# A decoder mixer step: memory prepared ahead of the x chunks, with constant matmuls on the scaled memory tiles

## The chip, the cores and the metric

One core of one Trainium2 chip runs the whole program. The metric is device time in microseconds (us) of one execution; a profiled execution gives the trace that the rows below come from.

## The reference

One layer of a hybrid mixer over 2048 prompt tokens and 8 x 4 sample tokens of width 1024:

```python
xn = rmsnorm(x, g_pre)
proj = xn @ w_in
a_c, b_c, g_c, x_r, g_r, q, g_q = split(proj)
mn = rmsnorm(mem, g_mem)                      # 256 memory tokens
mem_k, mem_v = mn @ w_mem_k, mn @ w_mem_v     # (256, 512) each
u = a_c * sigmoid(b_c)                        # conv group: depthwise conv of 31 taps, layernorm, silu
c = silu(layernorm(conv31(u))) * silu(g_c)
h = linear_recurrence(gates(conv4(x_r)))      # RG-LRU group
rr = h * silu(g_r)
o = softmax(q @ mem_k.T / sqrt(128)) @ mem_v * silu(g_q)
y = x + rmsnorm(concat(c, rr, o) @ w_out, g_post)
```

Keys and values of the memory are outputs too. Every product is made of three matmuls on split operands (high x high, high x low, low x high), in `mm3`.

## The kernel before

Phase 1 computes all projections in two parts of 1024 tokens; part 0 also carries the 32 sample tokens. A part is cut into chunks of 352, 352 and 320 tokens (the last has 352 columns with the samples). Phase 2 multiplies by `w_out`.

For part 0 the x rows come in as tiles of up to 128 rows (`chunk_rows`, three tiles a chunk, from the pool behind `big`). `norm_rows` takes the mean square of a tile on ScalarE (`row_rs`, L212), the power on GpSimd (L214) and scales the tile on VectorE (L220). `transposed` turns each 128-column block on TensorE (L227) into a PSUM bank of `ps_q`, which has four; ScalarE writes the high part (L229), VectorE the low part (L230), and the bank is free again. A projection (`proj`) loads one weight tile of 512 KB (`load_w`), splits it on ScalarE (L108) and VectorE (L109), and runs 24 matmuls for each chunk (L103 to L105). The raw weight tile `wr` has two buffers (`WR = 2`), and so have `wh` and `wl`: a third weight can be loaded when the first has been split.

The memory path is `mem_prep` (two tiles of 128 rows, the same norm, 16 transposes), `mem_k(h)` for four heads (a weight tile each, 24 matmuls of 256 columns) and `mem_v` (four weight tiles, 12 matmuls of 512 columns each, into two banks of `ps_q` that are held to the end).

Work is written in the order of the token string `ORDER`: G is a conv pair's projections and the convolution on VectorE, N, M and V are memory, X and S the recurrence, C, O, q, o gates and attention, L small constants, R row statistics. The Tile scheduler then places the instructions of all engines, by priority and by its own clock; each engine runs its list in that order. The x chunks of part 0 are prepared in a loop ahead of the string, and `G0` (weights 6 and 0, `FIRST` and `M_A`) follows. `WARM` gives 18 matmuls on a constant tile at the very start.

Of the kernel before, what the change touches and what calls it, by code (L numbers as in the profile page):

```python
# [16 lines left out]
P = 128  # L17
# [27 lines left out]
GRP = 2  # L45
NPB = 6
ORDER = (
    "G0 N M1 M0 M2 L X0 G1 G2:3 V G2 S0:2 S0:1 M3 S0:1 S0 C0 O0 C1 q0 G3 o0 R X1:7 X1 S1:1 G4 S1:1 S1:1 C2 C4 S1 O1 q1 o1 G5 q3 C3 q2 o2 o3 C5",
    "G0:1 G0 s0 s1 p v0 X0 v1 G1 S0:1 G2:1 S0:1 G2 S0:1 S0 C0 O0 q0 o0 G3 G4:3 X1 S1:1 G4 S1:1 S1 C1 O1 q1 G5 o1 q3 q2 o3 o2 C5 C4 C2 C3",
)  # L50
PART = 1024
SB8 = PART // P
WARM = 18
XRW = LH + PART + NB * (LH + NS)
M_A, M_B, M_GC, M_XR, M_GR, M_Q, M_GQ = 0, 6, 12, 18, 24, 30, 34
FIRST = M_B
# [11 lines left out]
def hybrid_mixer_kernel(ctx, tc, x, xT, mem, consts, lnc, ccT, lcT, ckT, cv, w_in,  # L68
# [3 lines left out]
    act, dve, pe, pool, sp = nc.scalar, nc.vector, nc.tensor, nc.gpsimd, nc.sync  # L72
# [21 lines left out]
    def bank(pl, w=512):  # L94
        t = pl.tile([P, 512], F32, tag="b", name="bk")
        return t[:, :w]

    warm = bank(ps_q, P)
    for _ in range(WARM):
        pe.matmul(warm, ones, ones, start=True, stop=True)  # L100

    def mm3(ps, lh, ll, rh, rl, first, last):
        pe.matmul(ps, lh, rh, start=first, stop=False)  # L103
        pe.matmul(ps, lh, rl, start=False, stop=False)  # L104
        pe.matmul(ps, ll, rh, start=False, stop=last)  # L105

    def split(hi, lo, src):
        act.activation(hi, src, AF.Copy)  # L108
        dve.tensor_tensor(lo, src, hi.bitcast(F32), op=ALU.subtract)  # L109
# [6 lines left out]
    def phase1():  # L116
# [17 lines left out]
        def lc(dt=F32):  # L134
            return pl.tile([P, 3, CW], dt, tag="lc", name="lc")
# [4 lines left out]
        def xslot(dt=F32):  # L140
            return pr.tile([P, XRW], dt, tag="xr", name="xr")

        cst = c1.tile([P, CST_W], F32, name="cst")

        def view(name, pat=None, **kw):
            o, w = CST[name]
            v = cst[:, o:o + w]
            return v.rearrange(pat, **kw) if pat else v
# [5 lines left out]
        V = {n: view(n) for n in VEC}  # L154
# [53 lines left out]
        def row_rs(t, n, junk):  # L208

            ms = pt.tile([P, 1], F32, tag="ms", name="ms")  # L210
            rs = pt.tile([P, 1], F32, tag="rs", name="rs")
            act.activation(junk()[:n, :D], t[:n, :D], AF.Square, accum_out=ms[:n, :])  # L212
            dve.tensor_scalar(rs[:n, :], ms[:n, :], 1.0 / D, EPS, op0=ALU.mult, op1=ALU.add)
            pool.tensor_tensor(rs[:n, :], rs[:n, :], mhalf[:n, 0:1], op=ALU.pow)  # L214
            return rs

        def norm_rows(tiles, junk):
            for t, n in tiles:
                rs = row_rs(t, n, junk)
                dve.tensor_scalar(t[:n, :D], t[:n, :D], rs[:n, :], None, op0=ALU.mult)  # L220

        def transposed(tiles, g, hi, lo):
            for k in range(KD):
                ps = bank(ps_q, sum(n for _, n in tiles))
                c0 = 0
                for t, n in tiles:
                    pe.transpose(ps[:, c0:c0 + n], t[:n, k * P:(k + 1) * P], ident[:n, :n])  # L227
                    c0 += n
                act.activation(hi(k), ps, AF.Copy, scale=g[:, k:k + 1])  # L229
                dve.scalar_tensor_tensor(lo(k), ps, g[:, k:k + 1], hi(k).bitcast(F32),  # L230
                                         op0=ALU.mult, op1=ALU.subtract)

        def load_w(src, ahead=None):
            with tc.high_priority(offset=W_HIGH if ahead is None else ahead):
                raw = pw.tile([P, KD, P], F32, tag="wr", name="wr", bufs=WR)
                sp.dma_start(raw, src)
                wh = pw.tile([P, KD, P], F32R, tag="wh", name="wh")
                wl = pw.tile([P, KD, P], F32R, tag="wl", name="wl")
                split(wh, wl, raw)
            return wh, wl  # L240
# [5 lines left out]

        def mem_prep():
            tiles = load_rows([[mem[i * P:(i + 1) * P, :]] for i in range(2)], flat_lc)
            norm_rows(tiles, xslot)
            mn = [lc(F32R).rearrange("p a b -> p (a b)")[:, :4 * NMEM].rearrange("p (a b) -> p a b", a=4)  # L250
                  for _ in range(4)]
            memn["hi"] = lambda k: mn[k // 4][:, k % 4, :]
            memn["lo"] = lambda k: mn[2 + k // 4][:, k % 4, :]
            transposed(tiles, gm, memn["hi"], memn["lo"])

        def mem_k(h):
            hi, lo = memn["hi"], memn["lo"]
            kv = pg.tile([P, 8, P], F32R, tag="g", name="kv")
            wh, wl = load_w(w_mem[h])
            ps = bank(ps_p, NMEM)  # L260
            for k in range(KD):
                mm3(ps, wh[:, k, :], wl[:, k, :], hi(k), lo(k), k == 0, k == KD - 1)
            f = ck()[:, :NMEM]
            act.activation(f, ps, AF.Copy)
            st_.dma_start(nkT[h], f)
            flat = lambda a: kv[:, a:a + 2, :].rearrange("p a b -> p (a b)")
            split(flat(0), flat(2), f)
            pool.dma_start(kvd[h][:, :4, :], kv[:, :4, :])

        def mem_v():  # L270

            hi, lo = memn["hi"], memn["lo"]
            ps = [bank(ps_q) for _ in range(2)]
            for i in range(HEADS):
                wh, wl = (t.rearrange("p a b -> p (a b)") for t in load_w(w_mem[HEADS + i]))
                for c in range(2):
                    cs = slice(c * P, (c + 1) * P)
                    for kk in range(2):
                        k = 2 * i + kk
                        ws = slice(kk * 512, kk * 512 + 512)  # L280
                        mm3(ps[c], hi(k)[:, cs], lo(k)[:, cs], wh[:, ws], wl[:, ws], k == 0, k == KD - 1)
                yield
            for c in range(2):
                f = big()[:, :512]
                act.activation(f, ps[c], AF.Copy)
                st_.dma_start(nv[c], f)
                kv = pg.tile([P, 8, P], F32R, tag="g", name="kv")
                split(kv[:, :4, :], kv[:, 4:, :], f.rearrange("p (h d) -> p h d", h=HEADS))
                for a in range(2):
                    pool.dma_start(kvd[:, :, 4 + 2 * a + c, :].rearrange("h p d -> p h d"), kv[:, 4 * a:4 * a + 4, :])  # L290
# [3 lines left out]
        for part in range(2):  # L294
            chunks = []
            for c0 in range(0, PART, CW):
                n = min(CW, PART - c0)
# [16 lines left out]
        def chunk_rows(part, c):  # L314
            return load_rows([[x[t:t + w, :] for _, w, t in b] for b in row_blocks(part, c)], big)
# [40 lines left out]
        for part in range(2):  # L356
            t0 = part * PART
            has_s = part == 0
            chunks = part_chunks[part]

            xh, xl = [], []
            ready = {}
            rows = {}
            if has_s:
                rows[0] = chunk_rows(0, 0)
                sp.dma_start(cst, consts)
            ready[FIRST] = load_w(w_in[FIRST], 0)
            for c, (c0, n, ns) in enumerate(chunks):
                h = px.tile([P, KD, CW], F32R, tag="xh", name="xh")
                l = px.tile([P, KD, CW], F32R, tag="xl", name="xl")  # L370
                w = n + ns
                hi, lo = (lambda k: h[:, k, :w]), (lambda k: l[:, k, :w])
                if has_s:
                    if c + 1 < len(chunks):
                        rows[c + 1] = chunk_rows(0, c + 1)
                    if c == 0:
                        ready[M_A] = load_w(w_in[M_A], 0)
                    norm_rows(rows[c], xslot)
                    transposed(rows.pop(c), gp, hi, lo)
                else:  # L380
                    split_cols(scaled_cols(part, c), gp, hi, lo)
                xh.append(h)
                xl.append(l)
            def proj(m, evac):
                wh, wl = ready.pop(m) if m in ready else load_w(w_in[m])
                for c, (c0, n, ns) in enumerate(chunks):
                    w = n + ns
                    ps = bank(ps_p, w)
                    for k in range(KD):
                        mm3(ps, wh[:, k, :], wl[:, k, :], xh[c][:, k, :w], xl[c][:, k, :w],  # L390
                            k == 0, k == KD - 1)
                    evac(c, ps)
                    yield
# [402 lines left out]
            for tok in ORDER[part].split():  # L796
                name, _, cnt = tok.partition(":")
# [252 lines left out]
```

## Time and profile before

| what | us |
|---|---|
| median of 3 runs | 1433.07 (1430.61 to 1433.35) |
| the profiled execution, its own time | 1434.65 |
| its span, first to last instruction | 1432.8 |
| TensorE (PE) busy | 1409.8 |
| VectorE (DVE) busy | 1097.3 |
| ScalarE (ACT) busy | 675.3 |
| GpSimd (POOL) busy | 158.4 |

A matmul's end is modelled and overlaps the next one, so TensorE's busy time hides a slow pace. What tells more is the count of matmuls in a stretch beside its length, and the granted clock there. The span lies 1.85 us below the execution's own time, which lies 1.58 us above the median.

### The profile page before, as it was taken

The numbers are of one execution on the slowest core, as the hardware profiler recorded it, in microseconds if no ns is written. First come the engines' busy times: TensorE is split into PE (matmuls) and PEld (weight loads), VectorE is DVE, ScalarE is ACT, GpSimd is POOL, SyncE is SP. The second block draws the span as 40 slices with busy tenths as digits, with TensorE's granted clock in tenths as the row PEclk, the third lists the DMA queues.
The fourth block names the chain that finished last, engine by engine and source line by source line (L and its number), as shares of the span: only waits on it lengthen the run. The fifth ranks groups of instructions, "written<-read, shape, count | busy, mean of one in ns | idle before, by whom it ended". The sixth has DMA issues, their size and how long they took to land. (4 is left out here: it accounts for less than half of the span.)

```text
span 1432.8 us, 20977 instructions
## 1 busy us (share of the span) xinstructions
PE 1409.8 (98%) x8346; PEld 1317.6 (92%) x8346; DVE 1097.3 (77%) x1481; ACT 675.3 (47%) x1314; POOL 158.4 (11%) x233
## 2 busy tenths in 40 slices
PE   8999999999999999999999999999999999999998
PEld 7899999999999999899999999999986788888886
DVE  6796995989978989599989997899864645545442
ACT  6423787336754335237842369434453432423321
POOL 2100222011210101012100121000100000000000
PEclk9999999999999999999999999999999999999999
DMA  7343526132252213631122211421474333324320
GB/s 225 110 46 89 140 90 227 42 93 72 85 188 75 65 60 111 219 123 66 54 104 65 75 54 60 162 74 53 154 238 128 96 121 124 125 85 140 98 86 30
DMA packets 102658, 152.24 MB, mean 106 GB/s; under 512 B 21368, under 2 KB 72176, under 8 KB 102560
## 3 DMA queue, kind: packets, MB, share of 16 engines
q1 hardware_dynamic: 89904, 118.66, 27.3%
q0 software_dynamic: 12656, 32.25, 6.7%
q8 instruction: 65, 1.06, 0.3%
q14 instruction: 33, 0.27, 0.1%
HBM read 114.84 MB, written 36.04 MB: 105 GB/s over the span
## 5 line engine op out<-in xcount | busy, mean ns | idle before, releaser
L103 PE MATMUL bk<-xh,wh 128*128 128x352 f32 (+1 forms) x1824 | 585.4, 322 | 2.1 <-ACT xh L229 1.3
L104 PE MATMUL bk<-xl,wh 128*128 128x352 f32 (+1 forms) x1824 | 585.2, 321 | 0.0
L105 PE MATMUL bk<-xh,wl 128*128 128x352 f32 (+1 forms) x1824 | 583.1, 321 | 0.0
L455 DVE SCALAR_TENSOR_TENSOR big<-ub,cst,big 128x1024 f32<-128x1024 f32 x360 | 457.4, 1284 | 8.5 <-issue 3.8
L104 PEld LDWEIGHTS bk<-xl,wh 128*128 128x128 f32 x1824 | 344.3, 189 | 2.7 <-issue 1.6
L103 PEld LDWEIGHTS bk<-xh,wh 128*128 128x128 f32 x1824 | 342.9, 188 | 4.2 <-ACT xh L229 1.9
L105 PEld LDWEIGHTS bk<-xh,wl 128*128 128x128 f32 x1824 | 343.2, 188 | 1.7 <-issue 1.0
L104 PE MATMUL bk<-wol,mh 128*128 128x512 f32 x512 | 201.1, 393 | 0.4 <-DVE wol L109 0.4
L103 PE MATMUL bk<-woh,mh 128*128 128x512 f32 x512 | 199.8, 392 | 0.0
L105 PE MATMUL bk<-woh,ml 128*128 128x512 f32 x512 | 199.4, 391 | 0.0
L108 ACT ACTIVATE wh<-wr 128x1024 fp32r<-128x1024 f32 x84 | 89.0, 1060 | 129.5 <-PE bk L104 113.7
L109 DVE TENSOR_TENSOR wl<-wr,wh 128x1024 fp32r<-128x1024 f32 x84 | 102.9, 1226 | 27.0 <-ACT wh L108 26.7
L105 PEld LDWEIGHTS bk<-woh,ml 128*128 128x128 f32 x512 | 96.2, 188 | 19.8 <-issue 0.8
L104 PEld LDWEIGHTS bk<-wol,mh 128*128 128x128 f32 x512 | 96.2, 188 | 19.6 <-DVE wol L109 0.8
L103 PEld LDWEIGHTS bk<-woh,mh 128*128 128x128 f32 x512 | 96.2, 188 | 19.4
L881 ACT ACTIVATE cr<-cr,lnv 128x128 f32<-128x128 f32 (+1 forms) x102 | 40.7, 477 | 151.1 <-DVE cr L879 151.1
L569 ACT ACTIVATE lc<-bk,hb 128x352 f32<-128x352 f32 (+3 forms) x144 | 77.3, 545 | 31.4 <-PE bk L105 29.3
L542 DVE SCALAR_TENSOR_TENSOR lc<-xr,cst,lc 128x352 f32<-128x352 f32 (+2 forms) x126 | 61.0, 521 | 7.2 <-ACT lc L538 7.1
L879 DVE TENSOR_TENSOR cr<-cr,bk 128x768 f32<-128x768 f32 (+1 forms) x17 | 15.6, 918 | 57.7 <-PE bk L878 57.7
L921 DVE TENSOR_TENSOR o<-bk,gpb 128x512 f32<-128x512 f32 (+1 forms) x34 | 23.3, 686 | 37.4 <-ACT sqj L920 37.4
L920 ACT ACTIVATE sqj<-bk 128x512 f32<-128x512 f32 (+1 forms) x34 | 20.1, 591 | 51.1 <-PE bk L105 50.8
L490 ACT ACTIVATE xr<-bk 128x352 f32<-128x352 f32 (+1 forms) x36 | 16.1, 450 | 56.4 <-PE bk L105 50.1
(238 smaller groups left out, 1693.6 us busy)
## 6 DMA issues: line engine op xcount, KB each, us to landing
wr<-in_w_in SPq DMA_DIRECT2D x76, 512.0 KB, 3.8
mr<-mixd SPq DMA_DIRECT2D x16, 1024.0 KB, 5.6
raw<-in_w_out SPq DMA_DIRECT2D x16, 512.0 KB, 4.6
xt<-in_x SPq DMA_DIRECT2D x16, 512.0 KB, 5.4
out_y<-xt SPq DMA_DIRECT2D x15, 512.0 KB, 2.7
convd<-big POOLq DMA_DIRECT2D x12, 512.0 KB, 3.7
mixd<-big POOLq DMA_DIRECT2D x12, 512.0 KB, 5.3
cr<-convd SPq DMA_DIRECT2D x16, 384.0 KB, 4.8
```

Source lines behind the costliest of these rows:

```text
L103: pe.matmul(ps, lh, rh, start=first, stop=False)
L104: pe.matmul(ps, lh, rl, start=False, stop=False)
L105: pe.matmul(ps, ll, rh, start=False, stop=last)
L108: act.activation(hi, src, AF.Copy)
L109: dve.tensor_tensor(lo, src, hi.bitcast(F32), op=ALU.subtract)
L455: dve.scalar_tensor_tensor(acc[:, :PART], ub[:, j:j + PART], cw[:, i, j:j + 1], acc[:, :PART], op0=ALU.mult, op1=ALU.add)
L490: act.activation(xb[:, LH + c0:LH + c0 + n], ps[:, :n], AF.Copy)
L542: dve.scalar_tensor_tensor(o, src(j), lw[:, ch, j:j + 1], o, op0=ALU.mult, op1=ALU.add)
L569: act.activation(dst[lo_:hi_, i, :], ps[lo_:hi_, :], AF.Tanh, scale=0.5, bias=hb[lo_:hi_, a, 3 * g + i:3 * g + i + 1])
L881: act.activation(cr[:, i, :], cr[:, i, :], AF.Silu, scale=lng[:, i:i + 1], bias=lnb[:, i:i + 1])
L920: act.activation(sqj[:m, :], ps[n][:m, :], AF.Square, scale=float(D ** -0.5), accum_out=ms[:m, n:n + 1])
L921: dve.tensor_tensor(o[:m, ns], ps[n][:m, :], gpb[:m, ns], op=ALU.mult)
```

## The change

The tokens N, M0 to M3 and V leave `ORDER`. A written order stands in their place ahead of the string in part 0: constants, memory rows, x rows of chunk 0, keys 0 and 1, x rows of chunk 1, chunk 0, keys 2 and 3, x rows of chunk 2, half the values, chunk 1, the rest of the values, the two weights of `G0`, chunk 2. `norm_rows` takes `keep`; for the memory tiles it issues five matmuls of 128 columns on each scaled tile into the bank of the start's constant matmuls, whose result nobody reads.

```diff
-    "G0 N M1 M0 M2 L X0 G1 G2:3 V G2 S0:2 S0:1 M3 S0:1 S0 C0 O0 C1 q0 G3 ...
+    "G0 L X0 G1 G2:3 G2 S0:2 S0:1 S0:1 S0 C0 O0 C1 q0 G3 ...
...
+KEEP = 5
...
-        def norm_rows(tiles, junk):
+        def norm_rows(tiles, junk, keep=0):
             for t, n in tiles:
                 rs = row_rs(t, n, junk)
                 dve.tensor_scalar(t[:n, :D], t[:n, :D], rs[:n, :], None, op0=ALU.mult)
+                for _ in range(keep):
+                    pe.matmul(warm, t[:n, :P], t[:n, :P], start=True, stop=True)
...
         def mem_prep():
             tiles = load_rows([[mem[i * P:(i + 1) * P, :]] for i in range(2)], flat_lc)
-            norm_rows(tiles, xslot)
+            norm_rows(tiles, xslot, KEEP)
...
-            if has_s:
-                rows[0] = chunk_rows(0, 0)
-                sp.dma_start(cst, consts)
-            ready[FIRST] = load_w(w_in[FIRST], 0)
-            for c, (c0, n, ns) in enumerate(chunks):
+
+            def x_chunk(c):
+                c0, n, ns = chunks[c]
...
-                    if c + 1 < len(chunks):
-                        rows[c + 1] = chunk_rows(0, c + 1)
-                    if c == 0:
-                        ready[M_A] = load_w(w_in[M_A], 0)
                     norm_rows(rows[c], xslot)
                     transposed(rows.pop(c), gp, hi, lo)
...
+            if has_s:
+                sp.dma_start(cst, consts)
+                mem_prep()
+                rows[0] = chunk_rows(0, 0)
+                mem_k(0)
+                mem_k(1)
+                rows[1] = chunk_rows(0, 1)
+                x_chunk(0)
+                mem_k(2)
+                mem_k(3)
+                rows[2] = chunk_rows(0, 2)
+                vals = mem_v()
+                next(vals)
+                next(vals)
+                x_chunk(1)
+                for _ in vals:
+                    pass
+                for m in (FIRST, M_A):
+                    ready[m] = load_w(w_in[m])
+                x_chunk(2)
+            else:
+                ready[FIRST] = load_w(w_in[FIRST], 0)
+                for c in range(len(chunks)):
+                    x_chunk(c)
```

The scheduler places everything anew. Three places show what became of the order.

SyncE's list of transfers at the start, before (`big` are x tiles, `lc` the memory tiles, `cst` the constants, `wr` weights; L203 loads rows, L236 weights):

```order
L203 DMA big<-in_x 128x1024 x2
L203 DMA big<-in_x 96x1024
L366 DMA cst<-in_consts 128x304
L236 DMA wr<-in_w_in 128x1024
L203 DMA big<-in_x 128x1024 x2
L203 DMA big<-in_x 96x1024
L236 DMA wr<-in_w_in 128x1024
L409 DMA ub<-in_ccT 128x8x30
L203 DMA lc<-in_mem 128x1024 x2
```

and now:

```order
L383 DMA cst<-in_consts 128x304
L204 DMA lc<-in_mem 128x1024 x2
L204 DMA big<-in_x 128x1024 x2
L204 DMA big<-in_x 96x1024
L239 DMA wr<-in_w_mem 128x1024 x2
L204 DMA big<-in_x 128x1024 x2
L204 DMA big<-in_x 96x1024
L432 DMA ub<-in_ccT 128x8x30 x3
L239 DMA wr<-in_w_mem 128x1024 x5
L204 DMA big<-in_x 128x1024 x2
L204 DMA big<-in_x 64x1024
L204 DMA big<-in_x 32x1024
```

The first projection weight was the fifth transfer; now it follows all eight memory weights and all x rows.

ScalarE's list at the start, before (L212 squares a tile, L108 splits a weight, L229 writes a transposed block):

```order
L212 ACTIVATE xr,ms<-big 128x1024 x2
L212 ACTIVATE xr,ms<-big 96x1024
L165 ACTIVATE spt<-spt 128x6
L108 ACTIVATE wh<-wr 128x1024
L212 ACTIVATE xr,ms<-big 128x1024
L229 ACTIVATE xh<-bk,cst 128x352 x4
```

and now (L213, L109 and L232 are the same three):

```order
L213 ACTIVATE xr,ms<-lc 128x1024 x2
L213 ACTIVATE xr,ms<-big 128x1024 x2
L213 ACTIVATE xr,ms<-big 96x1024
L232 ACTIVATE lc<-bk,cst 128x256 x4
L109 ACTIVATE wh<-wr 128x1024
L232 ACTIVATE lc<-bk,cst 128x256
L109 ACTIVATE wh<-wr 128x1024
```

The squares of the three x tiles of chunk 0 now stand between the memory's squares and the first block that is written from its transposes.

TensorE's list at the start, before (L100 the constant matmuls, L227 transposes, then projections):

```order
L100 MATMUL bk<-ones 128x128 x18
L227 MATMUL bk<-ident,big 128x128 x8
L227 MATMUL bk<-ident,big 128x96 x4
L103 MATMUL bk<-xh,wh 128x352
```

and now (L223 the ten new matmuls, L230 transposes, L104 to L106 the keys):

```order
L101 MATMUL bk<-ones 128x128 x18
L223 MATMUL bk<-lc 128x128 x5
L230 MATMUL bk<-ident,lc 128x128 x3
L223 MATMUL bk<-lc 128x128 x5
L230 MATMUL bk<-ident,lc 128x128 x11
L104 MATMUL bk<-lc,wh 128x256
L105 MATMUL bk<-lc,wh 128x256
L230 MATMUL bk<-ident,lc 128x128 x2
```

The first matmuls that count are now 256 columns wide and belong to the memory's keys.

## Rows read from the trace of the kernel before

**Rows 1.** The page: TensorE's share, and its busy tenths in 40 slices.
```profile
PE 1409.8 (98%) x8346; PEld 1317.6 (92%) x8346; DVE 1097.3 (77%) x1481; ACT 675.3 (47%) x1314; POOL 158.4 (11%) x233
PE   8999999999999999999999999999999999999998
```
**Rows 2.** Stretches of the start: length, then each engine's busy time (instructions); granted clock; DMA.
```profile
0.00:11.00 11.00, 7.06 (x44) 6.40 (x44) 3.42 (x18) 5.89 (x9) 2.68 (x12) 1.00 0.82 284
11.00:18.00 7.00, 6.00 (x23) 5.19 (x24) 6.72 (x25) 6.85 (x14) 1.92 (x3) 0.51 1.07 300
18.00:52.00 34.00, 31.39 (x208) 29.41 (x207) 23.13 (x60) 21.14 (x44) 3.43 (x6) 1.00 0.40 99
52.00:55.40 3.40, 3.40 (x18) 3.40 (x17) 3.40 (x6) 1.31 (x3) 0.57 (x1) 0.50 0.65 199
55.40:61.00 5.60, 4.04 (x32) 3.63 (x31) 4.88 (x6) 2.97 (x6) 0.58 (x1) 1.00 0.00 0
```
**Rows 3.** TensorE's waits, whole kernel: sum, times, longest (us).
```profile
PE bk L227 <- DVE big L220: 3.0, 2, 2.1
PE bk L105 <- DVE xr L663: 2.8, 2, 2.1
PE bk L904 <- DVE mh L109: 2.7, 1, 2.7
```
**Rows 4.** Timeline of the start: start, duration, instruction, idle before it and its end.
```profile
4.03 1.06 ACT L212 ACTIVATE xr<-big 128x1024 f32<-128x1024 f32 x1 [2.01 <-DMA big<-in_x]
...
8.33 1.06 ACT L212 ACTIVATE xr<-big 96x1024 f32<-96x1024 f32 x1 [1.86 <-DMA big<-in_x]
...
11.15 1.06 ACT L212 ACTIVATE xr<-big 128x1024 f32<-128x1024 f32 x1 [0.29 <-DMA big<-in_x]
...
12.79 0.66 PE L103 MATMUL bk<-xh,wh 128*128 128x352 f32 x1 [0.70 <-ACT xh L229]
```
**Rows 5.** Groups by shape from 0 to 61 us: busy, mean ns, idle before.
```profile
L103 PE MATMUL bk<-xh,wh 128*128 128x352 f32 x49 | 15.5, 346 | 2.1 <-ACT xh L229 1.3 <-ACT wh L108 0.7
L227 PE MATMUL bk<-ident,big 128*128 128x128 f32 x48 | 9.9, 295 | 2.7 <-DVE big L220 2.1 <-DVE xl L230 0.5
L212 ACT ACTIVATE xr<-big 128x1024 f32<-128x1024 f32 x6 | 6.4, 1060 | 4.0 <-DMA big<-in_x 3.8
L108 ACT ACTIVATE wh<-wr 128x1024 fp32r<-128x1024 f32 x6 | 6.3, 1054 | 2.8 <-PE bk L104 2.6 <-DMA wr<-in_w_in 0.2
L109 DVE TENSOR_TENSOR wl<-wr,wh 128x1024 fp32r<-128x1024 f32 x5 | 6.1, 1221 | 1.2 <-ACT wh L108 1.1
L100 PE MATMUL bk<-ones 128*128 128x128 f32 x36 | 5.8, 334 | 1.1 <-POOL ones L85 1.1
L103 PE MATMUL bk<-lc,wh 128*128 128x256 f32 x17 | 5.5, 331 | 1.0 <-ACT wh L108 0.8 <-ACT lc L229 0.2
L229 ACT ACTIVATE lc<-bk,cst 128x256 fp32r<-128x256 f32 x8 | 3.5, 489 | 6.0 <-PE bk L227 6.0
```
**Rows 6.** A dense stretch of 160 to 240 us, as in Rows 2.
```profile
160.00:240.00 80.00, 80.00 (x502) 79.85 (x501) 65.55 (x104) 67.43 (x116) 14.74 (x19) 1.00 0.42 131
```
**Rows 7.** Timeline of TensorE, three pairs of starts: transposes, keys, values.
```profile
22.58 0.46 PE L227 MATMUL bk<-ident,big 128*128 128x128 f32 x3
22.82 0.41 PE L104 MATMUL bk<-xl,wh 128*128 128x352 f32 x1
...
57.31 0.28 PE L103 MATMUL bk<-lc,wh 128*128 128x256 f32 x1
...
57.67 0.28 PE L103 MATMUL bk<-lc,wh 128*128 128x256 f32 x1
...
132.26 0.39 PE L103 MATMUL bk<-wh,lc 128*128 128x512 f32 x1
...
132.96 0.40 PE L103 MATMUL bk<-wh,lc 128*128 128x512 f32 x1
```
**Rows 8.** Weight loads of L236 in 0 to 80 us, from issue to landing.
```profile
DMA to landing us min/median/max: 3.7/6.4/11.4
```

More of the change, by code (lines that the diff above doesn't have):

```diff
@@ L47 @@
 ORDER = (
-    "G0 N M1 M0 M2 L X0 G1 G2:3 V G2 S0:2 S0:1 M3 S0:1 S0 C0 O0 C1 q0 G3 o0 R X1:7 X1 S1:1 G4 S1:1 S1:1 C2 C4 S1 O1 q1 o1 G5 q3 C3 q2 o2 o3 C5",
+    "G0 L X0 G1 G2:3 G2 S0:2 S0:1 S0:1 S0 C0 O0 C1 q0 G3 o0 R X1:7 X1 S1:1 G4 S1:1 S1:1 C2 C4 S1 O1 q1 o1 G5 q3 C3 q2 o2 o3 C5",
     "G0:1 G0 s0 s1 p v0 X0 v1 G1 S0:1 G2:1 S0:1 G2 S0:1 S0 C0 O0 q0 o0 G3 G4:3 X1 S1:1 G4 S1:1 S1 C1 O1 q1 G5 o1 q3 q2 o3 o2 C5 C4 C2 C3",
```

## The prediction

> **What bounds the kernel now.** The page comes first: TensorE is busy 98% of the span and 9 tenths or more in 38 of 40 slices [rows 1]. That number flatters it, since a matmul's recorded time overlaps the next one's, so I read the pace instead. In a dense stretch 502 matmuls fill 80 us, 0.159 us each for 352 columns [rows 6]. Three matmuls of the keys take 0.36 us, 0.120 each; three of the values 0.70 us, 0.233 each; a triple of transposes 0.24 us, 0.08 each [rows 7].
>
> Then the stretches of the start. From 0 to 61 us I count the work that is done, at that pace: six projection blocks of `G0` (two weights, three chunks, 24 matmuls: 144; the row counts 49 firsts of three, the last of which starts the next step) give 144 x 0.159 = 22.9; the memory's first keys, 50 matmuls (two heads and two more; 17 firsts in the row), 6.0; 24 triples of x transposes (48 wide ones in the row) 5.8; 16 memory transposes 1.3 [rows 5, 7]. The sum is 36.0 us of work in 60.8, so TensorE is **24.8 us late** when the start is over. Of these, 12.8 pass before the first matmul that counts [rows 4]; the clock is at 0.51 from 11 to 18 us and at 0.50 from 52 to 55.4, its lower level of 1.2 GHz, and there a busy engine gains half a microsecond per microsecond [rows 2]. The second dip and the holes after it fall on the memory step: 4.04 busy of 5.6, with a weight's split and its blocks awaited [rows 2, 5].
>
> Beyond the start little is lost: three waits hold 8.5 us together, one of them of the start [rows 3]. So what the change can move lies in the first 61 us, and at most 24.8 us of it.
>
> **What it removes and adds.** Nothing of the computation goes; 96 key and 48 value matmuls only move. Added are ten constant matmuls. At the start 18 such took 5.8 us, 0.32 each [rows 5], so ten cost 3.2 us if nothing hides them. They stand behind each memory tile's scaling, while ScalarE still squares x tiles, so I take 0; 3.2 is the other end, and a gain through the clock is a rival below.
>
> **The new start, step by step.** SyncE now issues constants, memory, three x tiles, then key weights. The third x tile is the sixth transfer, with as many bytes ahead of it as the sixth had before, which ended ScalarE's wait at 11.15 [rows 4]. ScalarE squares all three x tiles ahead of the first memory block. With the tile before it, the third square ends at some 12.5 (1.06 each and a read of the sum). Four blocks of 0.49 end at 14.5, the first weight's split of 1.05 at 15.5, a block at 16.0, the second split at 17.1 [rows 5]. TensorE's list has two matmuls of the first weight, two transposes, then two of the second: it is dense from 17.1, not from 12.8. By then 16 transposes and two matmuls are done, 1.5 us: 15.6 late.
>
> Between the constant matmuls and 17.1 TensorE has as little to do as it had before its first dip, so I expect 1.2 GHz from about 14 to 21 us, a dip as long as the first [rows 2]. Of that some 4 us are busy: 2 us more. Keys 0 and 1 and five triples end near 25, 17.6 late.
>
> Then each weight needs 1.05 us of ScalarE, 1.22 of VectorE and, through two buffers, at best 3.7 us to land [rows 5, 8]: 6.0 a pair by itself, against 24 x 0.120 = 2.9 or 12 x 0.233 = 2.8 us of TensorE for each weight, 5.7 a pair, and triples between. This pace nearly fits. I add 1.6 us for the waits where ScalarE, full from 8 to 49 us with nine squares, ten splits, 24 x blocks and the evacuations, hands over late. The values end at 46.1: done are 96 x 0.120 = 11.5, 48 x 0.233 = 11.2, memory transposes 1.3 and 12 triples 2.9, together 26.9, so 19.2 late. By then the first projection weight is split (landing 42.5, as the ninth weight, two turns behind the values' third), and `M_A` follows at 50, when 24 matmuls of chunk 0 are behind it. For the remaining blocks of chunks 1 and 2 I add 1.0.
>
> **The sum:** late before 24.8, now 20.2, a gain of 4.6 us. The rest I put at nothing: the string runs the same work, its convolutions only begin some 20 us later, and VectorE had 14.5 us free in 80 in a full stretch [rows 6]. If that cover is gone, a wait such as the one on `xr` at 2.8 us [rows 3] comes back once or twice: 0 to 5.6 us more, or 2.8 less if the new order removes the one there is. Against the profiled execution, 1434.65 us, this gives 1430.0; it lies 1.6 above the median of the runs, 1433.07, and so the forecast for the median is **1428.5**.
>
> **A rule against the change.** Over 160 to 240 us, the recurrence, ScalarE is busy 67.43 of 80 us and VectorE 65.55, and TensorE never pauses [rows 6]; in the old string V stood just ahead of it and M3 in it. The Trainium skill (Perfetto Trace Analysis, Identifying Performance Opportunities) advises interleaving regimes whose most contended engine differs; the change does the reverse. By that rule the recurrence would lose its cover, and the sum would be a rival's, the third below.
>
> **A rule on the loads.** In the first 18 us the transfers moved 284 and 300 GB/s [rows 2]. The Trainium skill (DMA: Bandwidth & Descriptors, Bandwidth) lists 341 GB/s for a transfer of 1 MB and 425 for 16 MB. By its lower figure I estimate that the sixth transfer would land 1.5 us earlier, and the sum would be 6.1 instead of 4.6. The trace disagrees, and I stay with its rate.
>
> **Rivals.**
>
> *The clock holds (faster still).* If the ten matmuls keep 2.4 GHz until the keys begin, the first dip's 2 us go. For it speaks that TensorE did only 1.3 us besides the constants in the first 11 us before [rows 2, 5], and now does more; against it that the hole to 15.5 remains. With it, and with ScalarE passing blocks at less than their 0.49 us since neighbours overlap, 32 blocks at 0.1 less, the gain is 4.6 + 2 + 3 = 9.6: 1423.5.
>
> *Two buffers too few (slower).* A weight tile landed after 3.7 us at best, but 6.4 in the median of this stretch [rows 8], where x rows shared the queue, and they do again. A pair of weights then takes 8.7 us, 2.7 more, four times over (keys 2 and 3, values 0 and 1, values 2 and 3, the two projection weights): 10.8 us, of which some 1.5 is slack in ScalarE's order. The gain turns into 4.7 us lost: 1437.8. It decides from a landing of 5.2 us on, where four turns cost 1.5 each and take the gain and the slack. Against it: in half of the turns the queue holds nothing but this one weight.
>
> *The gain is given back (no change).* V and M3 are 48 x 0.233 + 24 x 0.120 = 14.1 us of TensorE's work that no longer lies beside the recurrence. ScalarE and VectorE get rid there of five splits, 5.3 and 6.1 us, with them, so 12.6 us of ScalarE's idle time less 14.1 plus 5.3 leaves 3.8: full, but not over. If chains rather than sums decide, I count 4 us of new waits: 1432.5. It also covers a change that does little because `M_A` comes late by just what the memory saves.
>
> **How the numbers follow.** A measurement here tells apart about 0.2%, 2.9 us. The forecast (gain of 3 to 6.5) has 0.38, the clock holding 0.16, the gain given back 0.23, two buffers too few 0.23. Faster by over 0.2% is the first two, 0.54; within it the third, 0.23; slower the last, 0.23. The range runs from 1422, a little past the second case, to 1438, which takes in the last one's price; the 3.2 us of uncovered constant matmuls and the landing at its worst are left out.
>
> **What would show it.** Right: the first 256-column matmul at 15 to 16 us and density from 17; a granted clock near 0.5 from about 14 to 21 and full after; the values done at 46, the second dip at 52 gone; the first projection of chunk 0 at 46 to 47; no wait over 1 us at TensorE between 25 and 75 us. Wrong: ScalarE idle for weights that land after 5 us (two buffers); the clock full through 20 us (the first rival); new waits of TensorE on ScalarE or VectorE between 140 and 300 us (the third). The forecast is wrong altogether if the projections of chunk 0 begin after 52 us.

## The result and the profile after

The changed kernel takes **1443.11 us** (median of 8, 1441.06 to 1447.8), the kernel before 1433.53 on the same chip: ratio 1.0064 [1.0047, 1.008], so slower by 0.6%, where 1428.5 was forecast. By the medians the change costs 9.6 us. Its profiled execution took 1447.8 us (span 1446.0), at the upper end of its runs, and its span is 13.2 us longer than the one before; what stands below at one place can be some us more than in a typical execution. Of e8 and e12 below, one execution each took far longer (1986 and 2326 us) and is counted in the median; without it their medians are 1428.60 and 1428.37 us.

The page says as little as it did before [rows 1]: busy 98%.

```profile
PE 1413.1 (98%) x8366; PEld 1321.8 (91%) x8366; DVE 1097.3 (76%) x1481; ACT 678.7 (47%) x1314; POOL 157.6 (11%) x233
```

The stretches show more. First the changed kernel (columns as in [rows 2]), then the kernel before in the two stretches that were not shown:

```profile
11.00:18.00 7.00, 4.53 (x21) 3.11 (x20) 6.29 (x21) 6.80 (x14) 1.10 (x2) 0.76 1.12 316
18.00:40.00 22.00, 22.00 (x150) 20.71 (x150) 16.84 (x34) 16.14 (x32) 6.92 (x11) 0.92 0.78 247
40.00:52.00 12.00, 8.13 (x28) 5.77 (x27) 5.76 (x12) 5.29 (x9) 2.06 (x3) 0.72 0.74 209
52.00:61.00 9.00, 9.00 (x61) 8.96 (x60) 2.94 (x5) 4.46 (x9) 0.82 (x2) 0.99 0.19 62
240.00:260.00 20.00, 14.79 (x86) 14.51 (x85) 12.82 (x36) 11.60 (x20) 4.91 (x7) 0.83 0.49 178
400.00:445.00 45.00, 36.60 (x215) 35.90 (x214) 32.91 (x60) 24.18 (x39) 6.65 (x11) 0.89 0.49 151
```

```profile
240.00:260.00 20.00, 19.82 (x129) 19.27 (x128) 15.78 (x38) 13.58 (x34) 5.85 (x7) 1.00 0.39 134
400.00:445.00 45.00, 42.75 (x265) 42.15 (x265) 33.86 (x66) 23.86 (x51) 4.29 (x8) 0.96 0.50 161
```

From 240 to 260 us TensorE starts 86 matmuls where it started 129: 43 x 0.159 = 6.8 us. From 400 to 445 it starts 215 where it started 265; these are of several widths, and come to 6.9 us in the account below. Its waits, answering to [rows 3], name both places and a third in the start:

```profile
PE bk L104 <- ACT xr L685: 6.7, 2, 6.3
PE bk L104 <- ACT ub L445: 5.8, 2, 5.2
PE bk L104 <- ACT wh L109: 2.8, 1, 2.8
PE bk L230 <- DVE lc L233: 2.4, 1, 2.4
PE bk L104 <- DVE ck L115: 2.1, 1, 2.1
```

I keep the prediction's account, TensorE's lateness: the time less what all matmuls started by then would take at their steady pace, now counted over every matmul of the trace.

| stretch, us | late before, by its end | late after, by its end | lost more (+) |
|---|---|---|---|
| 0 to 61 | 24.6 | 25.4 | +0.8 |
| 61 to 240 | 26.1 | 26.5 | -0.4 |
| 240 to 260 | 26.9 | 34.3 | +7.0 |
| 260 to 400 | 27.6 | 35.0 | 0.0 |
| 400 to 445 | 32.1 | 46.4 | +6.9 |
| 445 to the end | 52.4 | 65.3 | -1.4 |

The sum is 12.9, against 13.2 us between the two spans. So there are three places: a start that gains nothing, and two stalls far behind it, in steps whose own code the change doesn't touch. The second stall is larger in this trace than it usually is: in the three other traces that keep both stalls (e1, e3 and e4 below, profiled in executions near their medians) the stretch of 400 to 445 us loses 7.6 to 8.2 us, not 11.4. That is some 3 us more than before instead of 6.9, and with it the table would come near the 9.6 us of the medians.

**The start.** The first key matmuls come at 15.40 and 16.71 us, as forecast (start, duration, instruction, idle before it and its end, here and in all timelines below):

```profile
13.89 1.54 PE L230 MATMUL bk<-ident,lc 128*128 128x128 f32 x6 [2.35 <-DVE lc L233]
15.40 0.58 PE L104 MATMUL bk<-lc,wh 128*128 128x256 f32 x1
...
16.71 0.58 PE L104 MATMUL bk<-lc,wh 128*128 128x256 f32 x1
```

Up to 40 us TensorE is 17.8 us late; from 40 to 52 it starts 28 matmuls (24.1 late at 50), with the clock at 0.72 of full speed. SyncE issued the last value weight (at 35.03) behind four transfers of x rows of chunk 2, and the projection weights behind that:

```profile
32.02 0.33 SPq L239 DMA_DIRECT2D wr<-in_w_mem  x1
32.44 2.18 SPq L204 DMA_DIRECT2D big<-in_x  x4
35.03 0.33 SPq L239 DMA_DIRECT2D wr<-in_w_mem  x1
38.98 0.33 SPq L239 DMA_DIRECT2D wr<-in_w_in  x1
```

Of the weights issued from 20 to 55 us this one took longest to land, 8.9 us:

```profile
DMA to landing us min/median/max: 3.6/4.5/8.9
```

ScalarE, in its list, then stands in the squares of these same x rows, and reaches the weight's split at 44.01; TensorE waited for it until 45.12. The weight itself landed at 43.9 (35.03 + 8.9), when the last square ended, so the landing alone would have held TensorE up about as long:

```profile
41.12 1.06 ACT L213 ACTIVATE xr<-big 128x1024 f32<-128x1024 f32 x1 [1.51 <-DMA big<-in_x]
...
42.83 1.06 ACT L213 ACTIVATE xr<-big 96x1024 f32<-96x1024 f32 x1 [0.55 <-DMA big<-in_x]
...
44.01 1.06 ACT L109 ACTIVATE wh<-wr 128x1024 fp32r<-128x1024 f32 x1
```

```profile
45.12 1.04 PE L104 MATMUL bk<-wh,lc 128*128 128x512 f32 x2 [2.80 <-ACT wh L109]
...
52.15 0.43 PE L104 MATMUL bk<-xh,wh 128*128 128x352 f32 x1
```

The last line is the first projection of chunk 0: the values' matmuls end just before it, at some 51.7 us.

**The stall at 249 us.** TensorE has filled the four projection banks (one of the conv pair, three of q) and needs one back. ScalarE frees a bank by its evacuation, the instruction that writes the finished block out of it; here that is the `tanh` of a conv pair (L445). Ahead of that in ScalarE's list stand four squares of the row statistics (L326), a weight's split (L109) and a table load:

```profile
241.68 1.04 ACT L326 ACTIVATE lc<-lc 128x1024 f32<-128x1024 f32 x1
...
242.72 1.04 ACT L326 ACTIVATE lc<-lc 128x1024 f32<-128x1024 f32 x1
...
243.76 1.04 ACT L109 ACTIVATE wh<-wr 128x1024 fp32r<-128x1024 f32 x1
244.71 1.04 ACT L326 ACTIVATE lc<-lc 128x1024 f32<-128x1024 f32 x1
...
245.75 1.04 ACT L326 ACTIVATE lc<-lc 128x1024 f32<-128x1024 f32 x1
...
246.90 1.28 ACT L445 ACT_TABLE_LOAD   x1
248.19 0.47 ACT L445 ACTIVATE ub<-bk 128x352 f32<-128x352 f32 x1
```

TensorE pauses for 5.21 us and then runs at half its pace, 0.29 us between starts, until shortly before 253.75, from where it is 0.16 again:

```profile
248.71 0.66 PE L104 MATMUL bk<-xh,wh 128*128 128x352 f32 x1 [5.21 <-ACT ub L445]
...
252.69 0.49 PE L105 MATMUL bk<-xl,wh 128*128 128x352 f32 x1
252.98 0.49 PE L106 MATMUL bk<-xh,wl 128*128 128x352 f32 x1
...
253.75 0.32 PE L106 MATMUL bk<-xh,wl 128*128 128x352 f32 x1
253.91 0.33 PE L104 MATMUL bk<-xh,wh 128*128 128x352 f32 x1
```

The kernel before has the same work there, but its last squares are over by 241.9, and the evacuations TensorE needs follow at 242.73 and 245.19:

```profile
240.72 1.06 ACT L323 ACTIVATE lc<-lc 128x1024 f32<-128x1024 f32 x1 [1.23 <-DMA lc<-in_x]
...
241.78 1.04 ACT L108 ACTIVATE wh<-wr 128x1024 fp32r<-128x1024 f32 x1
242.73 1.15 ACT L662 ACTIVATE xr<-bk 128x352 fp32r<-128x352 f32 x3
...
245.19 0.47 ACT L422 ACTIVATE ub<-bk 128x352 f32<-128x352 f32 x1
```

**The stall at 437 us.** TensorE waits for ScalarE's evacuation of q (L685), this for a buffer that VectorE frees (L643), and VectorE's list has three other things ahead of that: two scalings of part 1's x chunks (L349), one of which waits 1.23 us for its load, and a weight's low part (L110):

```profile
432.48 1.25 DVE L349 TENSOR_TENSOR lc<-lc,rb 128x1056 f32<-128x1056 f32 x1
433.65 1.21 DVE L110 TENSOR_TENSOR wl<-wr,wh 128x1024 fp32r<-128x1024 f32 x1
436.09 0.89 DVE L349 TENSOR_TENSOR lc<-lc,rb 128x704 f32<-128x704 f32 x1 [1.23 <-DMA lc<-in_xT]
436.90 0.39 DVE L643 SCALAR_TENSOR_TENSOR big<-big,xr 128x32 f32<-128x32 f32 x3
440.18 1.16 DVE L349 TENSOR_TENSOR lc<-lc,rb 128x960 f32<-128x960 f32 x1 [2.89 <-DMA lc<-in_xT]
...
441.69 1.38 DVE L686 SCALAR_TENSOR_TENSOR xr<-bk,xr 128x352 fp32r<-128x352 f32 x3
```

After the wait of 6.3 us follow one of 2.1 (for `ck`, behind the load of 440.18) and a dip of the clock, 0.89 over the stretch.

### The profile page after: what moved, and what is told of

It reads as the page before. It is cut to its first block, busy times and chain, and to the rows that moved or that the text cites. A ratio compares the mean times of both kernels' runs of the same rounds, so it can differ in the third digit from the quotient of the medians.

```text
span 1446.0 us, 21018 instructions
## 1 busy us (share of the span) xinstructions
PE 1413.1 (98%) x8366; PEld 1321.8 (91%) x8366; DVE 1097.3 (76%) x1481; ACT 678.7 (47%) x1314; POOL 157.6 (11%) x233
## 3 DMA queue, kind: packets, MB, share of 16 engines
q1 hardware_dynamic: 89904, 118.66, 26.5%
## 4 chain that ended last, share of the span: by engine, by line
PE 92%; DMA 3%; ACT 2%; DVE 1%; issue 1%; SPq 0%; DVEq 0%; POOLq 0%; ACTq 0%
PE bk L104 29%; PE bk L106 29%; PE bk L105 29%; DMA big<-in_x 1%; PE bk L927 1%; DMA lc<-in_xT 1%; PE bk L727 1%; DMA vs<-in_cv 1%; PE bk L763 0%; PE bk L230 0%; ACT lc L326 0%; DMA mixd<-kc 0%; ACT wh L109 0%; DVE xr L617 0%; ACT lc L592 0%
## 5 line engine op out<-in xcount | busy, mean ns | idle before, releaser
L104 PE MATMUL bk<-xh,wh 128*128 128x352 f32 (+1 forms) x1824 | 587.3, 322 | 7.9 <-ACT ub L445 5.8
L106 PE MATMUL bk<-xh,wl 128*128 128x352 f32 (+1 forms) x1824 | 584.6, 321 | 0.0
L104 PEld LDWEIGHTS bk<-xh,wh 128*128 128x128 f32 x1824 | 343.6, 188 | 10.3 <-ACT ub L445 6.3
L106 PEld LDWEIGHTS bk<-xh,wl 128*128 128x128 f32 x1824 | 343.5, 188 | 3.2 <-issue 2.5
L104 PE MATMUL bk<-woh,mh 128*128 128x512 f32 x512 | 200.2, 392 | 0.0
L106 PE MATMUL bk<-woh,ml 128*128 128x512 f32 x512 | 199.3, 390 | 0.0
L109 ACT ACTIVATE wh<-wr 128x1024 fp32r<-128x1024 f32 x84 | 89.1, 1060 | 118.3 <-PE bk L105 103.6
L110 DVE TENSOR_TENSOR wl<-wr,wh 128x1024 fp32r<-128x1024 f32 x84 | 104.2, 1240 | 35.5 <-ACT wh L109 34.2
L106 PEld LDWEIGHTS bk<-woh,ml 128*128 128x128 f32 x512 | 96.1, 188 | 19.8 <-issue 0.8
L104 PEld LDWEIGHTS bk<-woh,mh 128*128 128x128 f32 x512 | 96.2, 188 | 19.5
L565 DVE SCALAR_TENSOR_TENSOR lc<-xr,cst,lc 128x352 f32<-128x352 f32 (+2 forms) x126 | 61.0, 519 | 11.7 <-ACT lc L561 11.6
L943 ACT ACTIVATE sqj<-bk 128x512 f32<-128x512 f32 (+1 forms) x34 | 20.2, 593 | 46.9 <-PE bk L106 46.1
```

Of the source, the lines that this page charges most:

```text
L565: dve.scalar_tensor_tensor(o, src(j), lw[:, ch, j:j + 1], o, op0=ALU.mult, op1=ALU.add)
L943: act.activation(sqj[:m, :], ps[n][:m, :], AF.Square, scale=float(D ** -0.5), accum_out=ms[:m, n:n + 1])
```

## The experiments

Three theories. **Cover:** V and the fourth head's keys, 14.1 us of TensorE's work, no longer stand around the recurrence; TensorE gets there earlier than the other engines. **Order:** the stalls are accidents of the frozen lists, which any edit would move. **Start:** only the new start itself loses. Each ratio is to the kernel before on the same chip. The runs come from several chips, on which the median of the kernel before lay between 1433.53 and 1435.05 us, so a difference of medians between two runs carries up to 1.5 us of that:

| run | median us | ratio to before |
|---|---|---|
| e1_keep0 | 1443.75 | 1.0057 [1.0041, 1.0073] |
| e2_cover_back | 1429.63 | 0.9957 [0.9942, 0.9973] |
| e3_old_start_no_cover | 1445.01 | 1.0066 [1.005, 1.0083] |
| e4_weights_before_rows | 1440.75 | 1.004 [1.0027, 1.0053] |
| e5_values_back | 1434.62 | 0.9999 [0.9984, 1.0014] |
| e6_keys3_back | 1434.75 | 1.0 [0.9984, 1.0016] |
| e7_stats_later | 1437.64 | 1.0023 [1.0006, 1.0039] |
| e8_cover_back_keep0 | 1429.07 | 0.9958 [0.994, 0.9976] |
| e9_x2_big | 1437.91 | 1.0028 [1.0016, 1.0039] |
| e10_cover_back_x2_big | 1422.79 | 0.9916 [0.9902, 0.993] |
| e11_stats_later_x2_big | 1431.8 | 0.9984 [0.9971, 0.9998] |
| e12_before_x2_big | 1428.76 | 0.996 [0.9946, 0.9974] |
| e13_all_three | 1427.38 | 0.995 [0.9932, 0.9968] |

### The cover taken from the old start, and given back to the new one

In the kernel before (e3):

```diff
-    "G0 N M1 M0 M2 L X0 G1 G2:3 V G2 S0:2 S0:1 M3 S0:1 S0 C0 ...
+    "G0 N M1 M0 M2 M3 V L X0 G1 G2:3 G2 S0:2 S0:1 S0:1 S0 C0 ...
```

In the changed kernel (e2):

```diff
-    "G0 L X0 G1 G2:3 G2 S0:2 S0:1 S0:1 S0 C0 ...
+    "G0 L X0 G1 G2:3 V G2 S0:2 S0:1 M3 S0:1 S0 C0 ...
...
-                mem_k(3)
                 rows[2] = chunk_rows(0, 2)
-                vals = mem_v()
-                next(vals)
-                next(vals)
                 x_chunk(1)
-                for _ in vals:
-                    pass
```

> The kernel before with its own start, but all of the memory tokens (N, four M, V) put right behind G0, ahead of the recurrence: no new start, no constant matmuls, and no cover. Cover theory: a wait of TensorE of 4 to 6 us near 249 us, on the bank that the conv pair's evacuation frees, appears in it as in the changed kernel, and the time is 5 to 9 us above the kernel before: 1438 to 1443. Order theory and start theory: no such wait, within 3 us of the kernel before, 1430 to 1437.

> The changed kernel's start (constants, memory rows, keys 0 to 2 and the x chunks first), but V and the fourth head's keys back at their old tokens around the recurrence. Cover theory: TensorE's 5.2 us wait near 249 us and the clock dip with it are gone, about 7 us less than the changed kernel, and with the start's loss of 40 to 52 us gone too (no value weights there) 1428 to 1434 us. Order theory: the wait near 249 us stays or another of 3 us or more stands in its place between 150 and 300 us; 1437 to 1445. Start theory (the loss lies only in the first 61 us): about 3 us less than the changed kernel, 1439 to 1441, the wait at 249 as it is.

e3 has nothing of the new start and yet both stalls. Its waits of TensorE from 100 to 460 us (sum, times, longest):

```profile
PE bk L103 <- ACT ub L422: 5.2, 1, 5.2
PE bk L103 <- ACT xr L662: 5.0, 1, 5.0
```

It takes 1445.01 us, 2 more than the cover theory's upper end. e2 keeps the new start, less the values and the fourth head's keys, and has neither stall; one wait of 2.8 us is left, at the place where the kernel before waits 2.1 [rows 3]:

```profile
PE bk L106 <- DVE xr L680: 2.8, 1, 2.8
```

It takes 1429.63. In the account the stretch of 61 to 445 us loses 17 to 21 us without the cover (e1, e4, the changed kernel and e3, where 3 of the 21 lie before 100 us) and 8 with it (the kernel before and e2). So the cover decides both stalls, the early one and the one at 437 us, and the start theory falls as the whole cause. The 13.5 us between the medians of e2 and the changed kernel aren't the stalls alone: e2 also has no value weights in its start and is 19.4 us late at 61 us, not 25.4, so about 6 of them belong to the start. By that e2 is 5.4 us faster than the kernel before, which is 24.6 us late there.

### Which part of the cover

V alone at its old token (e5), and M3 alone (e6), each out of the order at the start:

```diff
-    "G0 L X0 G1 G2:3 G2 S0:2 S0:1 S0:1 S0 C0 ...
+    "G0 L X0 G1 G2:3 V G2 S0:2 S0:1 S0:1 S0 C0 ...
```

```diff
-    "G0 L X0 G1 G2:3 G2 S0:2 S0:1 S0:1 S0 C0 ...
+    "G0 L X0 G1 G2:3 G2 S0:2 S0:1 M3 S0:1 S0 C0 ...
```

> The changed kernel with only V back at its old token, ahead of the recurrence (48 matmuls of 0.233 us, 11.2 us); the fourth head's keys stay in the start. Cover as a sum (TensorE's lead over the recurrence is what is missing, 5.2 us of wait plus 2 us of low clock): 11.2 us is more than enough, the waits near 249 and 437 us are gone or under 2.5 us, and the time is that of the kernel with both back, 1429 to 1433. Cover as a place (filler is needed between the recurrence's own chunks): the wait of some 5 us stays, 1436 to 1441.

> The changed kernel with only the fourth head's keys back at their old token, between two chunks of the recurrence (24 matmuls of 0.120 us, 2.9 us); the values stay in the start. Cover as a sum: 2.9 of some 5.2 us of wait are covered, a wait of 2 to 3 us stays near 250 us, and the time is 3 us less than the changed kernel: 1438 to 1442. Cover as a place: the wait is gone, 1433 to 1437.

The sum is wrong in both; e6 comes out as the place theory has it, e5 (1434.62) between the two. M3, 2.9 us of TensorE, takes away a wait of 5.2 us and its dip (lateness 27.4 at 240, 28.2 at 260), and the later stall shrinks to 2.2 us. V, 11.2 us, leaves 3.0 us at 240 us, for q's evacuation, and 1.6 and 3.9 us at 424 and 430. The equal times hide this, since e5 also takes the values out of the start and is some 6 us earlier at 61 us. From 61 to 445 us e5 loses 16 us and e6 8: the smaller piece brings nearly all that the whole cover does. So TensorE's lead isn't simply paid off in microseconds: the scheduler freezes another order of ScalarE's list in each case (in e6 q's evacuation comes ahead of the `tanh`, in the changed kernel behind it). That cover acts by the order it leads to is only argued so far, and why the scheduler chose these orders isn't shown; the next run takes the order alone.

### The squares

```diff
-    "... C0 O0 C1 q0 G3 o0 R X1:7 X1 S1:1 G4 S1:1 S1:1 C2 ...
+    "... C0 O0 C1 q0 G3 o0 X1:7 X1 S1:1 G4 R S1:1 S1:1 C2 ...
```

> The changed kernel with the row statistics (R: eight squares of 1.04 us on ScalarE) written after G4 instead of ahead of the second group's X, so that no square stands on ScalarE ahead of the evacuation that TensorE waits for at 249 us. If ScalarE's order (squares ahead of the evacuation) makes that wait, it goes without any cover: 1434 to 1438. If the recurrence's chain itself is late, the wait of about 5 us stays at the same place, with ScalarE idle ahead of the evacuation: 1440 to 1445.

The stall at 249 is gone with no cover given back. TensorE's waits from 230 to 460 us, and ScalarE's evacuation, which now waits for the bank and not the bank for it:

```profile
PE bk L104 <- ACT xr L685: 4.8, 1, 4.8
PE bk L104 <- ACT ub L445: 0.6, 1, 0.6
```

```profile
242.12 0.47 ACT L445 ACTIVATE ub<-bk 128x352 f32<-128x352 f32 x1 [1.61 <-PE bk L106]
```

That is worth 5.5 us of the median. The squares ahead of the evacuation make this stall: with them out of the way the recurrence is in time, and three edits that leave them where they are (e1, e4, e9) keep a wait of 5.2 us. What the first line of the waits shows, 4.8 us at 429 us, is the other stall.

### The x loads of part 1

```diff
-            xs = [lc() for _ in range(3)]
+            xs = [big()[:, :3 * CW].rearrange("p (a b) -> p a b", a=3) if c else lc() for _ in range(3)]
```

In program order these buffers are last used by part 0's last steps, so the loads of chunks 1 and 2 come later, and VectorE's list has their scaling behind the second recurrence.

> The changed kernel with the transposed x tiles of chunks 1 and 2 of part 1 in buffers of the pool behind `big` instead of `lc`; these buffers come free later, so VectorE no longer stands behind the loads of these two chunks when the second recurrence ends. If VectorE's wait for these loads makes TensorE's stall near 437 us: it goes there (6.3 and 2.1 us of wait and the dip, 7 to 11 us of lateness between 400 and 445 us, to under 3), the stall near 249 stays, and the time is 1433 to 1437. If the second recurrence itself is late there: the stall stays over 4 us, 1440 to 1445. Loads that come too late for part 1 would show as waits of 3 us or more near 580 to 650 us.

> The kernel before with the move of part 1's x tiles alone, to see how much of that place it had lost itself (27.6 to 31.7 us late between 400 and 430 us). If VectorE's wait for the loads is the cause there too: 2 to 4 us faster than the kernel before, ratio 0.997 to 0.9985. If not: the same time.

```profile
PE bk L104 <- ACT ub L445: 5.2, 1, 5.2
PE bk L104 <- ACT xr L685: 1.8, 1, 1.8
```

e9 keeps the stall at 249, as it should, and the one near 437 falls from 6.3 and 2.1 us to 1.8 (e1, e4 and e7, without this edit, have 4.6 to 5.0 there). The account loses 4.1 us from 400 to 445 instead of 11.4; the median is 5.2 us below the changed kernel's, just above the range that was expected, and no wait over 1 us follows up to 700 us. e12 shows that the kernel before paid here too: its 4.5 us in that stretch fall to 0.1, and it is 5.6 us faster. The same stretch in it, 294 matmuls instead of 265:

```profile
400.00:445.00 45.00, 45.00 (x294) 44.71 (x293) 34.85 (x68) 26.73 (x56) 7.07 (x11) 1.00 0.37 120
```

So the change did not make this place; it made it dearer. The scalings in VectorE's list ahead of the recurrence's last steps, with their waits for loads, are shown as the cause of the greater part; how much of it is waiting and how much the scaling itself (2.1 us between 432.48 and 436.90) isn't told apart. Why 1.8 us remain without cover (2.5 in e11) isn't shown either. The trace of e9 has a candidate: chunk 0's tiles still use `lc`, and VectorE waits for them just ahead of the recurrence's last steps:

```profile
420.43 2.07 DVE L349 TENSOR_TENSOR lc<-lc,rb 128x1056 f32<-128x1056 f32 x2 [4.18 <-DMA lc<-in_xT]
```

e11 and e13 wait there too, 5.2 and 4.5 us; no run takes this wait away.

### Both, and the start by itself

e11 puts the edits of e7 and e9 together. e4 moves the x rows of chunk 2 in the changed kernel, and e13 does so in e11:

```diff
-                rows[2] = chunk_rows(0, 2)
                 vals = mem_v()
...
                 for m in (FIRST, M_A):
                     ready[m] = load_w(w_in[m])
+                rows[2] = chunk_rows(0, 2)
                 x_chunk(2)
```

> The changed kernel with both causes taken away and no cover given back: the row statistics after G4, and the x tiles of part 1's chunks 1 and 2 in `big`. If squares and loads are all that the missing cover costs, both stalls are gone and only the start's loss at 40 to 52 us is left: 1430 to 1433. If the recurrence without cover costs by itself, waits of 3 us or more remain between 150 and 450 us: 1436 to 1440.

> The changed kernel with the x rows of chunk 2 loaded after the weights of G0 instead of before the second half of the values, so that the last value weight and both projection weights no longer stand behind four x transfers in SyncE's queue. Start theory: TensorE's waits of 2.8 and 1.1 us at 45 to 48 us and the clock dip of 45 to 52 us are gone, TensorE is 18 to 20 us late at 61 us instead of 25.4, and the time falls by 4 to 6 us, to 1437 to 1439. Cover theory: the waits near 249 and 437 us stay or grow by what the start gives up (TensorE comes earlier to the same recurrence), and the time stays within 3 us of the changed kernel: 1440 to 1446. Order theory: the place of the waits after 200 us changes.

> The kernel with the row statistics later and part 1's x tiles of chunks 1 and 2 in `big` (1431.8 us), now also with the x rows of chunk 2 loaded after the weights of G0. If the x rows in SyncE's queue ahead of the last value weight and the two projection weights make the start's loss: the waits of 3.9 and 1.0 us at 45 to 50 us and the dip go, TensorE is 20 to 22 us late at 61 us instead of 27, half of it or less comes back by 100 us as waits for chunk 2, and the time is 1427 to 1430. If the start's gain is always given back to the late chunk 2: 1431 to 1433.

e11 takes 1431.8 us, as expected if squares and loads are nearly all that the missing cover costs; one wait of 2.5 us remains near 430. In e4 TensorE is 20.6 us late at 61 us, not 25.4, and the waits of 2.8 and 1.1 us are gone. But only 2.4 us of the median went (3.4 by the ratios), less than the start theory's 4 to 6: chunk 2's rows now come late (lateness 23.6 at 100 us, against 26.1 in the changed kernel), and both stalls are still there (5.2 and 5.0 us). e13, without the stalls but for a wait of 1.8 us near 422, shows the start's price by itself: 4.4 us less than e11 by the medians, 4.9 by the ratios, and 21.6 us late at 100 us instead of 28.0. The stretch of 40 to 52 us in it, with 70 matmuls instead of 28 and the clock full:

```profile
40.00:52.00 12.00, 11.59 (x70) 10.34 (x69) 6.93 (x10) 7.19 (x11) 4.08 (x6) 1.00 0.81 227
```

### The constant matmuls

```diff
-KEEP = 5
+KEEP = 0
```

> The changed kernel without the ten constant matmuls on the memory tiles (KEEP = 0); nothing else of the program text changes, but the scheduler places all engines anew. Cover theory (V and M3 no longer stand in the recurrence, so TensorE outruns it): the stalls of TensorE near 249 and 437 us stay, and the time stays within 3 us of the changed kernel's, 1440 to 1446; of the start, the first 256-column matmul comes as early or up to 1 us earlier. Order theory (the places of the stalls are accidents of one list): a small edit moves them, and the time differs by 4 us or more in either direction. Price of the matmuls in the prediction: 0 (bounds: 3.2 us gained to 2 us lost without them).

> The kernel with V and the fourth head's keys back at their old tokens, now without the ten constant matmuls. If these are covered and do nothing for the clock, within 1 us of that kernel's 1429.6; if they hold the clock up, 1 to 3 us above it, with a longer stretch at 1.2 GHz before 25 us; if they hold up the transposes, 1 to 3 us below.

e1 is 0.6 us above the changed kernel, e8 0.6 below e2, both within the intervals: the ten matmuls neither cost nor bring a time that these runs can tell. e1's edit reorders the start and leaves the stall at 249 with its 5.2 us, and the other with 4.6: against the order theory in the form that any edit moves the stalls.

### A version faster than both

> The kernel with V and the fourth head's keys back at their old tokens, with the same move of the x tiles of part 1's chunks 1 and 2. The lateness of 5.4 us between 400 and 430 us falls to 1 or 2: 1425 to 1427 against 1429.6 without. If the later loads cost as much elsewhere, 1428 to 1432.

e10, the new start with V and M3 at their old tokens and the x tiles in `big`, takes 1422.79 us, ratio 0.9916 [0.9902, 0.993] to the kernel before: better than expected, since the whole 5.1 us of that stretch goes (23.2 late at 400 and at 430) and nothing comes back by 560 (23.9).

## Why the prediction was wrong

*The account holds, the bound doesn't.* Lateness told where to look. But "beyond the start little is lost" was read from three rows of waits, which are five waits, and waits miss what a low clock costs. By the account the kernel before loses 27.8 us behind the start (24.6 late at 61 us, 52.4 at the end), 4.5 of them from 400 to 445, where e12 gains. So it was wrong that what the change can move lies in the first 61 us: nearly all that it cost lies behind them.

*The start up to 40 us: right.* First key matmuls at 15 to 16 us (15.40 and 16.71), 1.2 GHz from about 14 to 21 (0.76 over 11 to 18 us and 0.92 over 18 to 40: 1.7 / 0.5 = 3.4 and 1.8 / 0.5 = 3.5 us, together 6.9), 17.6 late near 25 (17.1). The third x tile landed at 11.7, where I had 11.15, and its square starts at 11.81. The Trainium skill's lower figure (DMA: Bandwidth & Descriptors, Bandwidth), by which I estimated a landing 1.5 us earlier, is not borne out.

*"The values end at 46.1", and `M_A` at 50 with 1.0 us to add: this step failed first.* I let the last weights come at a weight's own pace and said that in half of the turns the queue holds nothing else. In the turn that mattered it held four transfers of x rows, as the list of transfers ahead of the prediction already has it: 8.9 us to land instead of 3.7. The values ended at some 51.7 us, and the first projection of chunk 0 came at 52.15, past the 52 us from which the prediction called itself wrong altogether. Instead of 20.2 us late TensorE was 25.4 at 61 us. With the rows moved, it was 19.5 (e13) and 20.6 (e4); 2 to 3 us of that are lost again by 100 us to the late chunk 2, and but for these the rest of that sum was good. This is the rival *two buffers too few* in its mechanism, a landing over 5.2 us. But of nine landings three were as long (5.2, 8.9 and 6.4 us), and one of them held TensorE up, not four; its cause is the queue's order, not the number of buffers.

*"The rest I put at nothing": the step that cost most.* I argued that the work is the same and that VectorE had 14.5 us free in 80; for ScalarE the third rival had a sum too, 12.6 us idle, of which 3.8 would be left. A sum over 80 us says nothing of whether the one evacuation TensorE needs stands ahead of four squares of 1.04 us or behind them, or whether the recurrence's last step stands behind two scalings. Both stalls come from that sentence: 7.0 and, in the profiled execution, 6.9 us, where I allowed 0 to 5.6 in all. The rival *the gain is given back* named the right mechanism, V and M3 no longer beside the recurrence, and the right place for the first stall, but priced it at 4 us; one wait of 5.2 us and the 1.2 GHz behind it made 7. The second stall, at 437 us, is outside the 140 to 300 us where I would have looked, and rests on a place that was weak before: the 2.1 us wait on `xr` at 427 us [rows 3], which I counted as a possible gain.

*The rule on interleaving.* The Trainium skill (Perfetto Trace Analysis, Identifying Performance Opportunities) advises such interleaving. The runs bear out that cover mattered here, e2 and e3 from both sides: 8 us lost from 61 to 445 with it, 17 to 21 without. But e6 and e7 show that 2.9 us of it, or one moved row of squares, does as much for the stall at 249 us as the whole.

*The constant matmuls:* 0, as I took (e1, e8).

## What to carry to other kernels

When work is moved away from a stretch, don't ask only whether the other engines' sums still fit; list what stands, on each in-order engine, ahead of the one instruction that frees TensorE's next buffer, and look for long items without a deadline there (statistics, scaling of tiles that are needed far later). Here it paid to place such an item by hand behind the work that is waited for (e7), or to make it wait on a buffer that comes free late (e9, e12). And when loads are reordered, count for each late weight what the same queue issues right ahead of it.

## What was not expected of the hardware

A wait of 5.2 us cost 7: the clock went to 1.2 GHz in it, and 16 matmuls after it still ran 0.29 us apart instead of 0.16 (2.1 us). The stretch's 0.83 says the same: 0.17 x 20 / 0.5 = 6.8 us at the lower level.

The new start with the ten constant matmuls was profiled in ten kernels, the changed one among them, and the granted clock over 11 to 18 us came out between 0.71 (e13) and 1.00 (e2, e7, e9); without them it was 0.70 and 0.59 (e1, e8), with the old start 0.51 or 0.52. That they keep the clock up in some kernels fits this but isn't shown, since each kernel was profiled once and has lists of its own. The medians show nothing of it: in the three kernels that kept 2.4 GHz TensorE was 15.7 to 16.3 us late at 25 us, in e8, without them, 15.8.
